# A TensorE branch for experts of at most 32 tokens in layer 0 of a mixture-of-experts trunk, with ScalarE copying the first product's sums

## The chip, the cores and the metric

The kernel runs on one core of a Trainium2 chip. The metric is the device time of one execution in microseconds (us). A core has TensorE (PE; its weight loads are listed apart as PEld), VectorE (DVE), ScalarE (ACT), GpSimd (POOL) and SyncE (SP), which run their own instruction queues and wait for one another by semaphores; sixteen DMA engines move data between the core's memory and HBM.

## What is computed

The kernel computes a trunk of two layers on 1024 tokens of width 1024: a pooling mixer (layer 0) and a gated linear attention (layer 1), each followed by a mixture of 64 experts. Each token goes to the best of 8 groups and, in it, to the best two of 8 experts; an expert is a gated MLP with 384 hidden columns. Cut to the part around the change:

```python
def hier_moe(h, w_group, b_group, w_expert, b_expert, w_in, w_out):
    ...
    p_g, g_idx = lax.top_k(p_group, 1)
    ...
    p_top, e_idx = lax.top_k(p_e, MOE_TOP_E)
    weights = p_g * p_top / jnp.sum(p_top, axis=-1, keepdims=True)
    flat_id = (g_idx * MOE_EXPERTS_PER_GROUP + e_idx).reshape(-1)
    order = jnp.argsort(flat_id)
    token_of = order // MOE_TOP_E
    xs = t[token_of]
    group_sizes = jnp.bincount(flat_id, length=MOE_EXPERTS).astype(jnp.int32)
    gu = lax.ragged_dot(xs, w_in, group_sizes)
    gate, up = jnp.split(gu, 2, axis=-1)
    ys = lax.ragged_dot(jax.nn.silu(gate) * up, w_out, group_sizes)
    ys = ys * weights.reshape(-1)[order][:, None].astype(ys.dtype)
    out = jnp.zeros_like(t).at[token_of].add(ys)
```

A layer adds `gate2 * hier_moe(...)` to its input. 2048 pairs of token and expert are shared by 64 experts, 32 each on average; the weights of one expert are 1024x768 and 384x1024 float32, 4.7 MB.

## The kernel before

Layer 0 first makes its modulation vectors (`rows_use`, line 172: stationary 128x32, moving 128x384, sums on four groups of 32 PSUM partitions, one after the other), the pooling mixer and the routing. Then `moe` (line 624) goes over the experts, in layer 0 with the groups sorted by their number of tokens. The loop body names an expert by its position e, 0 to 63.

For each expert, up to 64 token rows are gathered (`gather`, 516, on GpSimd, two experts ahead, half rows of 512 columns on 128 partitions, so that 64 tokens fill them). `expert_in` (523) turns them with four TensorE transposes (528) and scales them into `xT` on ScalarE and VectorE (536, 538). `expert_first` (546) makes the first product: 16 matmuls of 128x384 with 64 stationary columns (64 tokens), gate columns of w_in into one half of the PSUM partitions and up columns into the other (554). The trace has two records for each such float32 matmul, hence 32. `expert_hidden` (558) is Silu of the gate half on ScalarE (561) and the product with the up half on VectorE (562). `expert_turn` (564) is three transposes (570) and a ScalarE copy (571). `expert_last` (573) is the product with w_out: six matmuls of 128x512, 12 records (579). `expert_add` (583) scales on VectorE (584) and adds the rows to `x_d` in HBM by an indirect DMA on GpSimd (585).

In layer 0, `expert_out` (590) puts TensorE's work in this order, which is kept as written: first product, the next expert's transposes (`between`), two filler units, the turn, two units, last product, four units. A unit (`piece`, 954) is three float16 matmuls of 128x512 (973) of layer 1's input projection; eight units make a 128x512 block that ScalarE evicts (975) and GpSimd's queue writes to HBM (976). Units exist from position 18 on, and run out now and then, before the next tile of 128 tokens is ready for them. Positions 2 to 15 have none and go through `expert_either` (602), as all experts of layer 1 do. Positions 0, 1 and 16 to 63 go through `expert_out`. After it, all engines but SyncE read the expert's count and branch (680): over 64 tokens, a second pass follows; otherwise it is jumped over, and TensorE adds what the pass would have added to its semaphore.

The weights of an expert take three of six slots of 1.5 MB (two for w_in, one for w_out), loaded by SyncE (`third_load`, 507, lines 513 and 514). The loads of expert e + 2 stand behind the branch of expert e, and each also waits for the load three before it.

Of the kernel before, what the change touches and what calls it, by code (L numbers as in the profile page):

```python
# [11 lines left out]
AF = mybir.ActivationFunctionType  # L12
OP = mybir.AluOpType
# [23 lines left out]
def trunk_kernel(ctx, tc, x_in, c_in, norm_gain, w_mod, b_mod, pool_w, pool_b, pool_scale,  # L37
# [20 lines left out]
    def part(slot, kb, n):  # L58
        a = int(kb * 256)
        return A[slot][:, a:a + n]  # L60

    def ps():
        return psum.tile([128, 512], F32, name="ps")
# [23 lines left out]
    cnt_i = cv(88)[0:1, :].bitcast(I32)  # L87
    wz_, isc_ = cv(128), cv(128)
    wz = wz_.rearrange("p (a b) -> p a b", a=8)
    zst = part(15, 11.25, 32).rearrange("p (b f) -> p b f", b=2)  # L90
    ig = cv(128).rearrange("p (a b) -> p a b", a=2).bitcast(I32)
    isc = isc_.rearrange("p (a b) -> p a b", a=2).bitcast(I32)
    wsl = cv(128).rearrange("p (a b) -> p a b", a=2)
# [1 line left out]
    so = small[:, 58:66].bitcast(I32)  # L95
    G2 = cv(512)
    gs = part(15, 11.5, 40)
    gmax, ginv, gmul, gadd = (gs[:, 8 * i:8 * i + 8] for i in range(4))
    gout = gs[:, 32:33]
    gtmp = gs[:, 33:37]  # L100
# [195 lines left out]
    def route_consts(area):  # L296

        ones_b, trim = as16(area("ones", 64)), as16(area("trim", 64))
        V.memset(ones_b, 1.0)
        V.tensor_tensor(trim, slot_no, pno.to_broadcast([128, 128]), op=OP.is_le)  # L300
        V.tensor_scalar(trim, trim, -1.0, None, op0=OP.mult)
        return ones_b, trim
# [220 lines left out]
    def expert_in(l, i, g, first=None):  # L523
        xT = part(15, 2 * i, 512).rearrange("p (c g t) -> p c g t", c=4, g=2)
        pp = [ps(), ps()]
        for cc in range(4):
            rows = XG[g].rearrange("p (r c) -> p c r", c=4)[:, cc] if l else XG[g][:, cc * 128:(cc + 1) * 128]
            T.transpose(pp[cc % 2][:, cc // 2 * 128:cc // 2 * 128 + 128], rows, ident)  # L528
        with tc.issue_after(first()) if first else ExitStack():
            for cc in range(4):  # L530
                pv = pp[cc % 2][:, cc // 2 * 128:cc // 2 * 128 + 128].rearrange("p (g t) -> p g t", g=2)
                for g in range(2):
                    kc = 4 * g + cc
                    sc, sh = modA[:, 0, 1, kc:kc + 1], sec(0, 3)[:, kc:kc + 1]
                    if cc % 2:
                        S.activation(xT[:, cc, g, :], pv[:, g, :], AF.Identity, bias=sh, scale=sc)  # L536
                    else:
                        ins = V.tensor_scalar(xT[:, cc, g, :], pv[:, g, :], sc, sh, op0=OP.mult, op1=OP.add).ins  # L538
        return ins
# [50 lines left out]
    def expert_out(l, i, sl, to, y, between=None, fill=lambda n: None):  # L590
        p1 = expert_first(i, sl)
        if between:
            between()
        fill(2)
        mark[:] = [expert_hidden(i, p1)]
        mark.append(expert_turn(i))
        fill(2)
        p2 = expert_last(i, sl)
        fill(4)
        expert_add(l, p2, *to, y)  # L600

    def expert_either(l, i, sl, to, y, nxt, many, to2, y2, aside):

        def hidden(b, p, n):
            if n:
                return expert_in(l, n[0], n[1], lambda: expert_hidden(b, p))
            return expert_hidden(b, p)

        p1 = expert_first(i, sl)
        with tc.If(many) as cmp:  # L610
            ins = hidden(i, p1, (i, y2))
            aside(ins, expert_turn(i))
            p2 = expert_last(i, sl)
            p1b = expert_first(i, sl, 1 - i)
            expert_add(l, p2, *to, y)
            hidden(1 - i, p1b, nxt)
            expert_turn(1 - i)
            expert_add(l, expert_last(1 - i, sl), *to2, y2)
        with cmp.Else():
            ins = hidden(i, p1, nxt)  # L620
            aside(ins, expert_turn(i))
            expert_add(l, expert_last(i, sl), *to, y)

    def moe(l, ring, mb, ob, load, ng, na, filler=None, before=None, aside=None, after=None):


        nr = len(ring)
        to = ig if l else isc
        pool_only = (ET.Pool,)

        def slots_at(e):
            return [ring[(3 * e + j) % nr] for j in range(3)]

        def count(e, engines):
            return nc.values_load(cnt_i[0:1, e:e + 1], engines=engines, min_val=0, max_val=SEQ,
                                  skip_runtime_bounds_check_because=COUNT_REASON)

        def main(e):
            return mb[e % len(mb)]

        def more(e):
            return ob[e % len(ob)]

        def ahead(e):
            if e < NE:
                with tc.If(count(e, pool_only) > 64):
                    gather(ig[:, 1, e:e + 1], more(e))

        for e in range(na):
            ahead(e)  # L650
        expert_in(l, 0, main(0))
        for e in range(NE):
            i = e % 2
            sl = slots_at(e)

            def between():
                if e + 1 < NE:
                    expert_in(l, 1 - i, main(e + 1))

            if before:  # L660
                before(e)
            if e + ng < NE:
                gather(ig[:, 0, e + ng:e + ng + 1], main(e + ng))
            tos = [(wsl[:, k, e:e + 1], to[:, k, e:e + 1]) for k in range(2)]
            engines = (ET.Pool, ET.Activation, ET.PE, ET.DVE)
            if l or 1 < e < NE // 4 and not units:
                ahead(e + na)
                expert_either(l, i, sl, tos[0], main(e), (1 - i, main(e + 1)) if e + 1 < NE else None,
                              count(e, engines) > 64, tos[1], more(e), aside or (lambda *marks: None))
                if after:  # L670
                    after(e)
            else:
                expert_out(l, i, sl, tos[0], main(e), between,
                           (lambda n: filler(e, n)) if filler else (lambda n: None))
                if aside:
                    aside(*mark)
                if after:
                    after(e)
                ahead(e + na)
                with tc.If(count(e, engines) > 64):  # L680
                    expert_in(l, i, more(e))
                    expert_out(l, i, sl, tos[1], more(e))
            for s in range(nr + 3 * e, min(nr + 3 * e + 3, 3 * NE)):
                load(s // 3, s % 3, slots_at(s // 3))
# [156 lines left out]
    def urgent(r):  # L841
        with tc.high_priority():
            next(r)
            next(r)
        next(r)

    urgent(route(0, 0, NT, area0, route_consts(area0)))
    gather(ig[:, 0, 0:1], 0)
    last = gather(ig[:, 0, 1:2], 1)
# [138 lines left out]
    def filler(e, n):  # L988
        if e < NE - 1:
            run_units(min(n, len(units) - 32) if e > NE - 6 else n)  # L990
# [474 lines left out]
```

## Time and profile before

| | us |
|---|---|
| median of 3 runs | 2311.88 |
| lowest and highest | 2305.32 to 2315.17 |
| the profiled execution | 2305.41 |
| its span, first to last instruction | 2303.7 |
| its granted TensorE clock, mean | 0.967 |

| engine | busy us | share of the span |
|---|---|---|
| PE | 1982.4 | 86% |
| PEld | 952.9 | 41% |
| DVE | 719.3 | 31% |
| ACT | 617.9 | 27% |
| POOL | 498.7 | 22% |

The busy time of an engine is the union of its instructions' times. The ends of matmuls are modelled, and records of matmuls overlap: the time from one start to the next is less than a record's duration. Branches, register loads and waits of an engine's sequencer aren't counted as busy; they are marked by a q (PEldq is TensorE's). A slice of the page is 57.6 us.

### The profile page before, as it was taken

The page shows a single profiled execution, that of the slowest core. Times are in us where ns is not written, and L with a number is a line of the kernel's source. Part 1 is how long each engine was busy: PE and PEld are TensorE (multiplying, and loading weights), DVE is VectorE, ACT ScalarE, POOL GpSimd, SP SyncE. Part 2 cuts the span into 40 slices and gives each one's busy share as a digit, 9 for nine tenths or more (in the row PEclk, how much of TensorE's full clock was granted, in tenths as well). Part 3 has the DMA queues.
Part 4 walks back from the last instruction along what each step waited for, and adds up shares of the span by engine and source line. Part 5 has one row for each costly group of instructions (what it writes and reads, how often), then busy time and mean ns, then how long its engine had stood idle before and what let it go on. Part 6 is the DMA issues. An engine that isn't in the chain of part 4 may idle for free. (4 is left out here: it accounts for less than half of the span.)

```text
span 2303.7 us, 31289 instructions
## 1 busy us (share of the span) xinstructions
PE 1982.4 (86%) x11197; PEld 952.9 (41%) x11198; DVE 719.3 (31%) x1760; ACT 617.9 (27%) x1418; POOL 498.7 (22%) x425
## 2 busy tenths in 40 slices
PE   7958888899999999998988999888887777778894
PEld 5644333344444444444434566533333333333341
DVE  3454545212111221211237666622221211122122
ACT  4222323222212221212125666312111111111113
POOL 0303222222222222222115110122222212122211
PEclk9979999999999999999998999999999999999997
DMA  9979989998988998999954952699999999999995
GB/s 349 365 302 383 394 302 345 373 341 326 347 309 296 336 359 321 369 337 360 349 169 143 332 192 89 238 388 406 406 398 392 404 388 402 396 398 389 400 385 191
DMA packets 173511, 770.07 MB, mean 334 GB/s; under 512 B 31711, under 2 KB 41357, under 8 KB 136382
## 3 DMA queue, kind: packets, MB, share of 16 engines
q1 hardware_dynamic: 127922, 684.66, 74.9%
q0 software_dynamic: 43952, 77.69, 12.3%
q10 hardware_dynamic: 1372, 4.28, 0.5%
q8 instruction: 155, 2.54, 0.4%
q14 instruction: 110, 0.90, 0.1%
HBM read 735.45 MB, written 69.80 MB: 350 GB/s over the span
## 5 line engine op out<-in xcount | busy, mean ns | idle before, releaser
L554 PE MATMUL ps<-slot,slot 128*64 128x384 f32 x4416 | 751.2, 490 | 77.2 <-DMA slot<-in_moe_w_in_dram 57.7
L554 PEld LDWEIGHTS ps<-slot,slot 128*64 128x64 f32 x4416 | 334.9, 137 | 494.9 <-issue 266.7
L579 PE MATMUL ps<-slot,slot 128*64 128x512 f32 x1656 | 403.3, 624 | 50.0 <-ACT slot L571 47.5
L561 ACT ACTIVATE slot<-ps 64x384 f32<-64x384 f32 x138 | 66.9, 485 | 1237.1 <-PE ps L554 1208.2
L973 PE MATMUL ps<-slot,slot 128*128 128x512 f16 x1152 | 278.9, 389 | 8.9 <-PEq L1110 5.6
L585 POOL DMA_INDIRECT x_d<-kept x96 | 159.4, 1661 | 544.5 <-DVEq L680 172.7
L538 DVE TENSOR_SCALAR slot<-ps,kept 128x64 f32<-128x64 f32 x552 | 151.1, 334 | 339.5 <-PE ps L528 338.1
L562 DVE TENSOR_TENSOR slot<-slot,ps 64x384 f32<-64x384 f32 x138 | 75.9, 550 | 504.9 <-ACT slot L561 504.2
L579 PEld LDWEIGHTS ps<-slot,slot 128*64 128x64 f32 x1656 | 110.7, 141 | 249.1 <-issue 183.8
L536 ACT ACTIVATE slot<-ps,kept 128x64 f32<-128x64 f32 x552 | 177.9, 402 | 66.5 <-PE ps L528 64.5
L584 DVE SCALAR_TENSOR_TENSOR kept<-ps,kept 128x512 f32<-128x512 f32 x96 | 72.0, 750 | 326.6 <-PE ps L579 323.8
L973 PEld LDWEIGHTS <-slot 128*128 128x128 f16 x1152 | 108.1, 100 | 156.6 <-issue 50.3
L517 POOL DMA_INDIRECT kept<-h_d,kept x96 | 102.2, 1065 | 307.4 <-DMA x_d<-kept 189.2
L570 PE MATMUL ps<-kept,slot 64*128 64x64 f32 x414 | 75.9, 290 | 85.7 <-DVE slot L562 84.2
L585 POOL DMA_INDIRECT x_d<-slot,kept x42 | 66.9, 1592 | 352.2 <-DVE slot L584 158.3
L570 PEld LDWEIGHTS ps<-kept,slot 64*128 64x128 f32 x414 | 57.9, 202 | 126.3 <-DVE slot L562 93.1
L1285 PE MATMUL ps<-slot,slot 128*128 128x512 f16 x384 | 85.7, 379 | 1.2 <-DVE slot L1277 0.9
L584 DVE SCALAR_TENSOR_TENSOR slot<-ps,kept 128x512 f32<-128x512 f32 x42 | 31.5, 751 | 124.3 <-PE ps L579 118.3
L528 PEld LDWEIGHTS ps<-kept 128*128 128x128 f32 x384 | 44.6, 163 | 61.4 <-issue 60.8
L528 PE MATMUL ps<-kept 128*128 128x128 f32 x384 | 65.8, 294 | 4.5 <-DMA kept<-h_d,kept 4.5
L1285 PEld LDWEIGHTS <-slot 128*128 128x128 f16 x384 | 37.1, 98 | 46.7 <-issue 2.1
L571 ACT COPY slot<-ps 128x192 f32<-128x192 f32 x138 | 44.6, 323 | 32.1 <-PE ps L570 32.1
(343 smaller groups left out, 1681.9 us busy)
## 6 DMA issues: line engine op xcount, KB each, us to landing
slot<-in_moe_w_in_dram SPq DMA_DIRECT2D x256, 1536.0 KB, 12.3
slot<-in_moe_w_out_dram SPq DMA_DIRECT2D x128, 1536.0 KB, 12.8
slot<-in_w_mod_dram SPq DMA_DIRECT2D x24, 1536.0 KB, 11.2
slot<-in_gla_w_in_dram SPq DMA_DIRECT2D x8, 1536.0 KB, 8.4
slot<-in_w_mod_dram SPq DMA_DIRECT2D x8, 1152.0 KB, 7.8
h_d<-slot POOLq DMA_DIRECT2D x16, 512.0 KB, 5.7
slot<-in_x_dram SPq DMA_DIRECT2D x8, 512.0 KB, 11.6
slot<-x_d POOLq DMA_DIRECT2D x8, 512.0 KB, 7.5
```

The source lines that it names most:

```text
L517: return G.indirect_dma_start(out=XG[i], out_offset=None, in_=hv, in_offset=bass.IndirectOffsetOnAxis(ap=idx, axis=0), bounds_check=2 * SE ...
L528: T.transpose(pp[cc % 2][:, cc // 2 * 128:cc // 2 * 128 + 128], rows, ident)
L536: S.activation(xT[:, cc, g, :], pv[:, g, :], AF.Identity, bias=sh, scale=sc)
L538: ins = V.tensor_scalar(xT[:, cc, g, :], pv[:, g, :], sc, sh, op0=OP.mult, op1=OP.add).ins
L554: T.matmul(p1[s, 0:384], xT[:, cc, g, :], W[:, u], start=n == 0, stop=n == 7)
L562: return V.tensor_tensor(hh, hh, p1[up, 0:384], op=OP.mult).ins
L570: T.transpose(p3[:, cc * 64:(cc + 1) * 64], hh[:, :, cc], ident[s, s])
L579: T.matmul(p2[g * 64:g * 64 + 64, :], hT[:, cc * 64:(cc + 1) * 64], o[:, cc, g * 512:(g + 1) * 512], start=cc == 0, stop=cc == 2)
L584: V.scalar_tensor_tensor(XG[y], p2, w, G2, op0=OP.mult, op1=OP.mult)
L585: ins = G.indirect_dma_start(out=yv[l], out_offset=bass.IndirectOffsetOnAxis(ap=sidx, axis=0), in_=XG[y], in_offset=None, bounds_check=2 * ...
L973: T.matmul(p, hP[:, m, kc, :], W[:, n, :], start=kc + i == 0, stop=kc == KC - 1 and i == 2)
L1285: T.matmul(p, oT[:, m, kc, :], woh[kc][:, n, half * 512:(half + 1) * 512], start=kc + i == 0, stop=kc == KC - 1 and i == 2)
```

## The change

In layer 0, `expert_out`'s first pass becomes `expert_few`. On TensorE alone, the count of the expert is compared with 32 twice. With at most 32 tokens, the first product uses 32 stationary columns and four groups of 32 PSUM partitions (gate and up, each with its even and odd parts of the contraction); otherwise it is done as before. ScalarE copies the 128x384 sums to SBUF (`pc`), ahead of the next expert's scaling. The turn is made of the sums, not of the hidden rows: with at most 32 tokens by three matmuls with the matrix `pick`, which adds even and odd parts while it turns; otherwise by three transposes. Silu (ScalarE) and the product (VectorE) then work on the turned sums, 128x192. Second passes, `expert_either` and layer 1 stay as they are. `pick` is made once; a small staging buffer (`zst`) moves to another place.

```diff
-    zst = part(15, 11.25, 32).rearrange("p (b f) -> p b f", b=2)
+    zst = part(15, 11.6875, 32).rearrange("p (b f) -> p b f", b=2)
...
+    pick = part(15, 11, 128)
...
+    def first_of(few, i, sl):
+        p1 = ps()
+        xT = part(15, 2 * i, 512).rearrange("p (c g t) -> p c g t", c=4, g=2)
+
+        def weights(g, cc, u):
+            return A[sl[g]].rearrange("p (k u f) -> p k u f", k=4, u=2)[:, cc, u]
+
+        with tc.If(few) as cmp:
+            for n in range(4):
+                for u in range(2):
+                    for odd in range(2):
+                        g, cc = n // 2, n % 2 * 2 + odd
+                        q = 32 * (2 * u + odd)
+                        T.matmul(p1[q:q + 32, 0:384], xT[:, cc, g, 0:32], weights(g, cc, u), start=n == 0, stop=n == 3)
+        with cmp.Else():
+            for n in range(8):
+                for u in range(2):
+                    T.matmul(p1[64 * u:64 * u + 64, 0:384], xT[:, n % 4, n // 4, :], weights(n // 4, n % 4, u),
+                             start=n == 0, stop=n == 7)
+        return p1
+
+    def turn_of(few, b, pc):
+        pv = pc.rearrange("p (r c) -> p r c", c=3)
+        hT = part(15, 5.5 + 0.75 * b, 192).rearrange("p (c t) -> p c t", c=3)
+        p3 = ps()
+        with tc.If(few) as cmp:
+            for cc in range(3):
+                T.matmul(p3[:, cc * 128:(cc + 1) * 128], pv[:, :, cc], pick, start=True, stop=True)
+        with cmp.Else():
+            for cc in range(3):
+                T.transpose(p3[:, cc * 128:(cc + 1) * 128], pv[:, :, cc], ident)
+        p3v = p3[:, 0:384].rearrange("p (c u t) -> p c u t", c=3, u=2)
+        S.activation(hT, p3v[:, :, 0], AF.Silu)
+        return V.tensor_tensor(hT, hT, p3v[:, :, 1], op=OP.mult).ins
+
+    def expert_few(l, i, sl, to, y, few, between, fill):
+        p1 = first_of(few, i, sl)
+        pc = part(15, 4, 384)
+
+        def copy():
+            mark[:] = [S.copy(pc, p1[:, 0:384]).ins]
+            return mark[0]
+
+        between(copy)
+        fill(2)
+        mark.append(turn_of(few, i, pc))
+        fill(2)
+        p2 = expert_last(i, sl)
+        fill(4)
+        expert_add(l, p2, *to, y)
...
+        few = {}
+
+        def few_next(e):
+            if e < NE and e not in few:
+                few[e] = count(e, (ET.PE,)) <= 32
...
-            def between():
+            def between(first):
                 if e + 1 < NE:
-                    expert_in(l, 1 - i, main(e + 1))
+                    expert_in(l, 1 - i, main(e + 1), first)
+                else:
+                    first()
...
-                expert_out(l, i, sl, tos[0], main(e), between,
-                           (lambda n: filler(e, n)) if filler else (lambda n: None))
+                few_next(e)
+                expert_few(l, i, sl, tos[0], main(e), few.pop(e), between, lambda n: filler(e, n))
...
                 ahead(e + na)
+                few_next(e + 1)
                 with tc.If(count(e, engines) > 64):
...
+    V.memset(pick, 0.0)
+    sides_of = "p (u h t) -> p u h t"
+    V.tensor_tensor(pick.rearrange(sides_of, u=2, h=2)[:, :, 0], ident.rearrange(sides_of, u=2, h=2)[:, :, 0],
+                    ident.rearrange(sides_of, u=2, h=2)[:, :, 1], op=OP.add)
```

## Rows read from the trace of the kernel before

**Rows 1.** The page: an engine's busy time, and GB/s in 40 slices.
```profile
PE 1982.4 (86%) x11197; PEld 952.9 (41%) x11198; DVE 719.3 (31%) x1760; ACT 617.9 (27%) x1418; POOL 498.7 (22%) x425
...
GB/s 349 365 302 383 394 302 345 373 341 326 347 309 296 336 359 321 369 337 360 349 169 143 332 192 89 238 388 406 406 398 392 404 388 402 396 398 389 400 385 191
```

**Rows 2.** Stretches: length, each engine's busy time, granted clock, DMA share, GB/s.
```profile
250.00:300.00 50.00, 40.03 (x217) 16.89 (x219) 25.92 (x50) 15.88 (x35) 13.23 (x10) 1.00 1.02 387
452.40:1149.60 697.20, 656.96 (x3420) 296.15 (x3420) 135.82 (x343) 162.19 (x397) 156.02 (x142) 0.99 0.91 337
468.60:529.80 61.20, 58.51 (x300) 25.69 (x301) 10.40 (x27) 14.77 (x35) 14.18 (x13) 1.00 0.94 348
1600.00:1700.00 100.00, 90.02 (x503) 39.57 (x499) 22.11 (x56) 18.35 (x56) 23.79 (x18) 1.00 1.01 403
```

**Rows 3.** Timeline of PE, one expert with units: start, us, instructions, idle before.
```profile
483.82 5.38 PE L554 MATMUL ps<-slot,slot 128*64 128x384 f32 x32 [0.30 <-PEq L680]
489.13 0.66 PE L528 MATMUL ps<-kept 128*128 128x128 f32 x4
489.62 1.46 PE L973 MATMUL ps<-slot,slot 128*128 128x512 f16 x6
491.55 0.53 PE L570 MATMUL ps<-kept,slot 64*128 64x64 f32 x3 [0.47 <-DVE slot L562]
492.01 1.47 PE L973 MATMUL ps<-slot,slot 128*128 128x512 f16 x6
493.41 2.79 PE L579 MATMUL ps<-slot,slot 128*64 128x512 f32 x12
496.14 2.76 PE L973 MATMUL ps<-slot,slot 128*128 128x512 f16 x12
499.20 1.19 PE L554 MATMUL ps<-slot,slot 128*64 128x384 f32 x6 [0.30 <-PEq L680]
```

**Rows 4.** PE's waits, 452.4 to 1149.6 us: total us, times, longest.
```profile
PE ps L570 <- DVE slot L562: 23.2, 44, 1.8
PE ps L554 <- PEq L680: 12.5, 42, 0.4
```

**Rows 5.** DMA issues and median landing, 452.4 to 1149.6; last two: 250 to 300.
```profile
slot<-in_moe_w_in_dram SPq DMA_DIRECT2D x90, 1536.0 KB, 9.4
...
x_d<-kept POOLq DMA_INDIRECT x45, 4.9
kept<-h_d,kept POOLq DMA_INDIRECT x44, 6.4
...
kept<-h_d,kept POOLq DMA_INDIRECT x4, 7.8
x_d<-kept POOLq DMA_INDIRECT x3, 8.0
```

**Rows 6.** Waits of SyncE's queue, 452.4 to 1149.6 us.
```profile
SPq L513 <- PEq L680: 317.4, 44, 14.4
```

**Rows 7.** Timeline of PE: one burst of modulation matmuls (line 180).
```profile
81.89 2.79 PE L180 MATMUL ps<-slot,slot 128*32 128x384 f32 x32
```

**Rows 8.** Timeline of PE: full matmuls of 128 columns in the pooling mixer.
```profile
16.52 2.23 PE L783 MATMUL ps<-slot,slot 128*128 128x128 f32 x14
```

**Rows 9.** Lines 610 and 680, TensorE's branches: ns min/median/max, first and last start.
```profile
L610 PEldq COMPARE_BRANCH  x87: 65/213/361, 214.9 to 2268.4; - x87
L680 PEldq COMPARE_BRANCH  x51: 70/217/360, 192.8 to 1157.8; - x51
```

**Rows 10.** Groups by line, ACT, whole span: copies from PSUM.
```profile
L571 ACT COPY slot<-ps 128x192 f32<-128x192 f32 x138 | 44.6, 323 | 32.1 <-PE ps L570 32.1
L187 ACT COPY slot<-ps 128x384 f32<-128x384 f32 x5 | 2.3, 478 | 18.7 <-PE ps L180 18.7
```

**Rows 11.** Timeline of PE: positions 49 (three filler matmuls) and 51, the starts.
```profile
948.66 5.38 PE L554 MATMUL ps<-slot,slot 128*64 128x384 f32 x32 [0.30 <-PEq L680]
...
974.78 1.51 PE L554 MATMUL ps<-slot,slot 128*64 128x384 f32 x8 [0.30 <-PEq L680]
```

## The prediction

> **What bounds the kernel now.** I read the page first: TensorE is busy for 86% of the span, and the memory traffic runs near 400 GB/s in the last third but mostly between 300 and 380 in slices 6 to 20, where layer 0's experts run [rows 1]. The table of stretches separates the two: in layer 1 (1600 to 1700 us) the transfers are full (share 1.01, 403 GB/s) and TensorE has gaps; while layer 0 mixes experts with filler matmuls (452.4 to 1149.6 us), TensorE is busy for 657 of 697 us at a granted clock of 0.99 and the transfers stand at a share of 0.91 and 337 GB/s [rows 2]. So this stretch is TensorE's, with a small reserve in the transfers. The timeline of one expert there is its whole budget [rows 3]: first product 5.31 us (483.82 to 489.13), transposes 0.49, two filler units with a wait of 0.47, the turn of the hidden rows 0.46, two units 1.40, the last product 2.73, four units and a gap of 0.30, together 15.38 us. Of TensorE's waits in the stretch two matter: 23.2 us for the hidden product on VectorE, 12.5 us at the end of an expert [rows 4]. The weights don't make it wait: a half of w_in lands 9.4 us after its issue [rows 5], and SyncE issues an expert's loads only when TensorE leaves the expert two before it (317.4 us of waiting in 44 times) [rows 6], so that they have one expert's length, 15.4 us, and arrive some 6 us early.
>
> **How many experts change.** The new code serves positions 0, 1 and 16 to 63. The reference's routing of its own inputs, sorted by group size as the kernel sorts them, gives at most 32 tokens at 38 of these 50: 18, 20, 21, 23 to 30, 32 to 38, 40, 42 to 50, 53, 55 to 63, all in the stretch. Of the 38, 30 have all filler units; 42, 49, 50, 57, 58, 61, 62 and 63 have nearly none. Twelve of the 50 take the other branch.
>
> **First product.** 32 records stay 32 records of 384 columns, on four column groups instead of two. The trace has that very form: the modulation matmuls of line 180, 32 records of 128x384 with 32 weight columns, cycling through the four groups as the new loop does, took 2.79 us, three times alike, against 5.38 [rows 3, 7]. Saving: 2.59 us. The Trainium skill's page "TensorE: Matmul & The Clock Gate", section "Part 3: Packing small matmuls", lists measured speedups of 3.07 for four row tiles and 2.38 for three column tiles, less than the number of tiles. By 3.07 against a full two, the product would take an estimated 3.5 us and save 1.9; the row of the same form speaks against it here, and no run yet shows the form inside an expert.
>
> **Turn.** The small branch has three full matmuls of 128 columns, six records instead of three. Fourteen records of that form took 2.23 us [rows 8], 0.112 us from one to the next, so six cost 0.67 against 0.46: +0.21. The other branch's three transposes of 128 columns are one record each, about +0.05.
>
> **Two branches on TensorE.** Branches on its queue took 65 to 361 ns: the low end where the code falls through, the high one where it jumps [rows 9]. The count's register load comes before the old branch, which TensorE's queue covers. The first branch stands right behind the old one's end, where TensorE has run empty (the 0.30 gap), so it is exposed: 0.17 us for the fall-through of small experts (0.07 and one step), 0.4 for the jump of the others; between 0 and 0.4. The jump at the end of the body and the second branch have filler or product work queued ahead: 0. If that cover is gone, 0.3 each. Does the end of a branch empty TensorE, as that of the old one does? That one adds to TensorE's own semaphore because its skipped side has fewer matmuls; here both sides have as many (16, and 3), so I take 0, with 0.4 for each of the two as the upper bound.
>
> **The path from first to last product.** Today: Silu, four VectorE scalings, the product, the turn, a copy. New: a copy of 128x384 (478 ns), then the turn; and behind it Silu and product on 128x192, some 323 ns each by the copy of that size [rows 10]. The first part, 0.48 and two handovers, is covered by transposes and two units (1.9 us); so the wait of 0.24 to 0.5 per expert goes: -0.3. The second, about 0.9 us, is covered by two units (1.40); without units it shows 0.5 more than the copy's 0.41 of today. The copy waits where the Silu waited, with the four scalings and, at times, a unit's eviction behind it on ScalarE; the next one waiting for those is the next expert's first product, a dozen us away. The scalings on VectorE no longer stand ahead of what TensorE waits for. The matrix pick is made once, by two VectorE instructions ahead of the routing, and a small buffer moves to free its place: at most 1 us on the whole. No transfer and no SyncE or GpSimd step is moved in the code; but loads start when TensorE leaves an expert, so they start sooner.
>
> **Small expert with filler, TensorE alone:** -2.59 + 0.21 + 0.17 - 0.3 = -2.5 us, from 15.4 to 12.9. The others: +0.4 - 0.3, about 0.
>
> **What is late next: the transfers.** Four such experts moved 348 GB/s x 61.2 us = 21.3 MB, 5.3 MB each [rows 2]. At the 387 GB/s of layer 0's own full stretch (250 to 300 us) that is 13.8 us, at layer 1's 403 it is 13.2; by the share, 0.94 of 15.3 us at a full 1.02, it is 14.1. I take 13.7. So 12.9 can't be held: each expert eats 0.8 us of the lead, which is 12.9 - 9.4 = 3.5 us [rows 5], and after four in a row the transfers set the pace. The 30 stand in runs of 1, 2, 8, 7, 1, 6, 1, 2 and 2: 21 in the first four of a run (2.5 each: 52 us), 9 behind (1.7 each: 15). The eight without units take 13.1 us now (two of them 948.66 to 974.78) [rows 11], about the transfers' own need (5.0 MB at 390 GB/s is 12.8): 2 us in all, at most 20. Sum 69. From the other side: 697 us at a share of 0.91 can't fall below 622 at 1.02, 75 us; the eight larger experts between 18 and 63 go on at 15.4 with about 1.2 us idle transfers each, leaving 65. Both can't be met without loss where the two engines alternate; I take 60 us, nearer the cap. The profiled execution took 2305.4 us (span 2303.7 and 1.7 around it), 6.5 under the median of three, 2311.9; 60 off it is 2245, and off the median 2252.
>
> **Rivals.**
> 1. The branches' ends empty TensorE: 0.8 more per expert. The small ones then take 13.7, where the transfers would hold many of them anyway: 30 x 1.7 less 12 x 0.8 is 41 us, 2271. For: the 0.30 gap behind the old branch. Against: equal counts.
> 2. The gathers come late. An expert's row gather is issued only after the scatter-add of the expert three before it has landed; the landings are 4.9 and 6.4 us, 8.0 and 7.8 when the transfers are full [rows 5], so 15.8 with some 1.5 for issuing. The rows are needed 1.5 + 12.9 + 2.8 = 17.2 us after that scatter-add starts: just met. A us late on each of 30 costs 30: 2282. Spills on GpSimd's queue stand in between.
> 3. Slower: the jumps stall on code. If one jump in three (some 33 of 100) waited for code as long as the shortest landing, 4.9 us, that is 162 us lost against 60: 2414; it decides from 0.6 us per jump. Against: the old branches jump over a whole second pass in at most 0.36 us [rows 9]. The Trainium skill's page "Runtime: NRT & Kernel Launch", section "Instruction fetch mechanics", has this rule: a taken branch whose target lies outside the fetched window waits for a transfer. Its effect isn't seen in these rows.
> 4. The change doesn't do what it says: hardly any expert takes the small side, or the groups don't overlap there. Then 50 x 0.1 to 0.4 is lost, 2317 to 2332, or the gain is below 12.
> 5. The transfers do better than today's share says (403 GB/s throughout): 85 us, 2227.
>
> **Chances:** forecast 0.64 (2234 to 2267), rival 1 0.12, rival 2 0.10, rival 3 0.04, rival 4 0.07, rival 5 0.03. About 0.5% (12 us) can be told from no change. Faster by more: forecast, 1, 2 and 5 less a little for their tails, 0.87; within: 0.07; slower: 0.06. The range takes in rivals 1, 2 and nearly 5: 2230 to 2293.
>
> **What would show it.** Small experts: the first product as 32 records of 32 weight columns in about 2.8 us, the whole expert in 12.9 to 13.7; larger ones 5.4 and 15.4. Within runs of small experts, waits of the first product for w_in or of the transposes for gathers appear, the share rises to about 1.0, and the wait for VectorE at the turn vanishes in experts with units. The next layer stays as it is. Wrong would be: a first product above 3.5 us, gaps of over 0.5 us behind either branch, or a stretch whose share stays at 0.91 while TensorE waits.

## The result, and the profile after

The changed kernel took 2258.0 us (median of 4 runs, 2251.0 to 2265.5) against 2308.6 for the kernel before beside it (4 runs): a ratio of 0.977, interval 0.975 to 0.980, 51 us faster. Predicted were 2252, with 2230 to 2293 around it. The profiled execution took 2258.2 us with a span of 2256.5, 47.2 less than before's.

In its profile line 618 is the first product of a small expert (at most 32 tokens) and 622 that of a larger one; 633 and 636 are their turns, 646 the copy of the sums, 638 Silu, 639 the product, 580 the last product, 1041 a filler unit, 1043 ScalarE's eviction of a filler block, 744 the old branch, 612 and 631 the two new ones.

TensorE's timeline shows a small expert with units, and further up two rows of a larger one; the columns are those of [rows 3]:

```profile
473.45 5.38 PE L622 MATMUL ps<-slot,slot 128*64 128x384 f32 x32 [0.58 <-PEq L744]
...
481.22 0.61 PE L636 MATMUL ps<-kept,slot 128*128 128x128 f32 x3 [0.50 <-ACT slot L646]
...
575.35 2.79 PE L618 MATMUL ps<-slot,slot 128*32 128x384 f32 x32 [0.48 <-PEq L744]
578.07 0.65 PE L529 MATMUL ps<-kept 128*128 128x128 f32 x4
578.56 1.46 PE L1041 MATMUL ps<-slot,slot 128*128 128x512 f16 x6
580.52 1.31 PE L633 MATMUL ps<-slot 128*128 128x128 f32 x6 [0.50 <-ACT slot L646]
581.66 1.46 PE L1041 MATMUL ps<-slot,slot 128*128 128x512 f16 x6
583.05 2.79 PE L580 MATMUL ps<-slot,slot 128*64 128x512 f32 x12
585.78 2.76 PE L1041 MATMUL ps<-slot,slot 128*128 128x512 f16 x12
588.97 1.50 PE L618 MATMUL ps<-slot,slot 128*32 128x384 f32 x16 [0.42 <-PEq L744]
```

From start to start, against [rows 3]:

| step | before, us | after, us | predicted change | change |
|---|---|---|---|---|
| first product | 5.31 | 2.72 | -2.59 | -2.59 |
| transposes | 0.49 | 0.49 | 0 | 0 |
| two units and the wait at the turn | 1.93 | 1.96 | -0.3 | +0.03 |
| turn | 0.46 | 1.14 | +0.21 | +0.68 |
| two units | 1.40 | 1.39 | 0 | -0.01 |
| last product | 2.73 | 2.73 | 0 | 0 |
| four units and the gap at the end | 3.06 | 3.19 | +0.17 | +0.13 |
| sum | 15.38 | 13.62 | -2.5 | -1.76 |

So the first product came as computed, and so did the branch. The turn cost three times its surcharge, and the wait in front of it is still there; only the one who is waited for has changed, from VectorE's hidden product to ScalarE's copy. TensorE's waits in the stretch say it for all experts (columns as in [rows 4]; then the stretch itself, columns as in [rows 2]):

```profile
PE ps L633 <- ACT slot L646: 19.2, 30, 1.3
PE ps L618 <- PEq L744: 14.3, 33, 0.5
PE ps L580 <- DVE slot L639: 13.4, 11, 2.6
PE ps L618 <- DMA slot<-in_moe_w_in_dram: 5.6, 6, 2.3
...
PE ps L636 <- ACT slot L646: 3.5, 7, 0.5
```

```profile
452.00:1110.00 658.00, 594.12 (x3581) 269.75 (x3581) 130.19 (x345) 167.55 (x407) 158.37 (x144) 0.98 0.97 363
```

The transfers went from a share of 0.91 to 0.97 and from 337 to 363 GB/s [rows 2], but the first product waited for weights only 6 times, 5.6 us together. SyncE's queue waited for the old branch for 317.4 us before [rows 6] and now does so for less. It also waits for earlier loads to land, as it did before. First a row of the kernel before (452.4 to 1149.6 us), then two of the kernel after (452 to 1110):

```profile
SPq L513 <- DMA slot<-in_moe_w_in_dram: 239.7, 44, 7.3
```

```profile
SPq L514 <- PEq L744: 247.6, 44, 12.6
SPq L514 <- DMA slot<-in_moe_w_in_dram: 217.8, 51, 8.2
```

**Why the turn waits and is long.** ScalarE's timeline in the same expert, and two groups of instructions by line (busy us, mean ns of one, idle before):

```profile
579.41 0.69 ACT L1043 ACTIVATE slot<-ps,slot 128x512 f32<-128x512 f32 x1 [10.88 <-PE ps L1041]
579.99 0.47 ACT L646 COPY slot<-ps 128x384 f32<-128x384 f32 x1
580.35 1.31 ACT L537 ACTIVATE slot<-ps,kept 128x64 f32<-128x64 f32 x4
581.86 0.33 ACT L638 ACTIVATE slot<-ps 128x192 f32<-128x192 f32 x1 [0.21 <-issue]
```

```profile
L633 PEld LDWEIGHTS ps<-slot 128*128 128x128 f32 x228 | 42.9, 260 | 35.9 <-ACT slot L646 35.2
L646 ACT COPY slot<-ps 128x384 f32<-128x384 f32 x50 | 23.6, 473 | 51.2 <-PE ps L622 29.5 <-PE ps L618 20.2 <-PE ps L529 1.4
```

ScalarE has stood idle for 10.9 us, and the sums have been there since 578.1. But its queue holds the eviction of a filler block first, which must wait for the units behind the transposes; the copy comes behind it, 1.85 us after the sums, though in the code it stands ahead. So it is in 24 of the 30 small experts with units; in the other six no block is completed there. And each weight load of the turn takes 260 ns: `pc` is read with a step of three elements. The costs of the branches are small, as predicted:

```profile
L612 PEldq COMPARE_BRANCH  x88: 67/176/1256, 185.7 to 1108.0; - x88
```

**Where the 47 us are.** By the starts of the first products in the two profiles:

| part | before, us | after, us | change |
|---|---|---|---|
| ahead of position 0 | 183.4 | 190.2 | +6.8 |
| positions 0 and 1 | 29.0 | 28.0 | -1.0 |
| positions 2 to 15 | 212.5 | 213.4 | +0.9 |
| positions 16 to 62 | 724.7 | 672.6 | -52.1 |
| position 63 and all behind it | 1154.1 | 1152.4 | -1.7 |

Of the 52.1, the 30 small experts with units hold -55.4 (1.85 each), the eight larger ones +1.5, the seven small ones without units +1.4, positions 16 and 17 +0.4. The 6.8 ahead of position 0 belong to that one execution: in the profiles of the eight experiments below, with the same code there, position 0 starts at 171.9 to 182.5 us.

### The profile page after: what moved, and what is told of

It is laid out like the page before. It is cut to its first block, busy times and chain, and to the rows that moved or that the text cites. A ratio compares the mean times of both kernels' runs of the same rounds, so it can differ in the third digit from the quotient of the medians.

```text
span 2256.5 us, 31745 instructions
## 1 busy us (share of the span) xinstructions
PE 1912.5 (85%) x11311; PEld 924.9 (41%) x11312; DVE 710.4 (31%) x1762; ACT 621.8 (28%) x1425; POOL 498.6 (22%) x425
## 3 DMA queue, kind: packets, MB, share of 16 engines
q8 instruction: 170, 2.79, 0.5%
## 5 line engine op out<-in xcount | busy, mean ns | idle before, releaser
L555 PE MATMUL ps<-slot,slot 128*64 128x384 f32 x2816 | 482.2, 491 | 63.7 <-DMA slot<-in_moe_w_in_dram 58.3
L555 PEld LDWEIGHTS ps<-slot,slot 128*64 128x64 f32 x2816 | 204.9, 138 | 350.3 <-issue 233.2
L1041 PE MATMUL ps<-slot,slot 128*128 128x512 f16 x1152 | 273.5, 383 | 7.3 <-DVEq L1178 5.8
L562 ACT ACTIVATE slot<-ps 64x384 f32<-64x384 f32 x88 | 42.7, 485 | 753.9 <-PE ps L555 718.1
L580 PEld LDWEIGHTS ps<-slot,slot 128*64 128x64 f32 x1656 | 111.5, 141 | 264.1 <-issue 169.9
L563 DVE TENSOR_TENSOR slot<-slot,ps 64x384 f32<-64x384 f32 x88 | 48.6, 552 | 499.5 <-ACT slot L562 494.5
L1041 PEld LDWEIGHTS <-slot 128*128 128x128 f16 x1152 | 112.4, 101 | 150.5 <-issue 44.6
L1043 ACT ACTIVATE slot<-ps,slot 128x512 f32<-128x512 f32 x48 | 32.7, 686 | 415.3 <-PE ps L1041 409.4
L618 PE MATMUL ps<-slot,slot 128*32 128x384 f32 x1216 | 107.2, 488 | 21.3 <-PEq L744 14.3
L571 PE MATMUL ps<-kept,slot 64*128 64x64 f32 x264 | 49.0, 293 | 56.0 <-DVE slot L563 53.0
L1353 PE MATMUL ps<-slot,slot 128*128 128x512 f16 x384 | 85.7, 379 | 1.2 <-DVE slot L1345 0.9
L618 PEld LDWEIGHTS ps<-slot,slot 128*32 128x32 f32 x1216 | 42.6, 109 | 79.0 <-issue 64.3
L622 PE MATMUL ps<-slot,slot 128*64 128x384 f32 x384 | 66.7, 501 | 9.0 <-PEq L744 5.5
```

The costliest lines, as they stand in the source:

```text
L555: T.matmul(p1[s, 0:384], xT[:, cc, g, :], W[:, u], start=n == 0, stop=n == 7)
L571: T.transpose(p3[:, cc * 64:(cc + 1) * 64], hh[:, :, cc], ident[s, s])
L580: T.matmul(p2[g * 64:g * 64 + 64, :], hT[:, cc * 64:(cc + 1) * 64], o[:, cc, g * 512:(g + 1) * 512], start=cc == 0, stop=cc == 2)
L618: T.matmul(p1[q:q + 32, 0:384], xT[:, cc, g, 0:32], weights(g, cc, u), start=n == 0, stop=n == 3)
L622: T.matmul(p1[64 * u:64 * u + 64, 0:384], xT[:, n % 4, n // 4, :], weights(n // 4, n % 4, u), start=n == 0, stop=n == 7)
L1041: T.matmul(p, hP[:, m, kc, :], W[:, n, :], start=kc + i == 0, stop=kc == KC - 1 and i == 2)
```

## Experiments

Each ratio is against the kernel before on the same chip (2303.9 us, 10 runs, for the first four; 2306.7, 11 runs, for the others). Beside the kernel after it took 2308.6, so differences between kernels are given by the ratios below (0.001 is 2.3 us), not by the medians. They carry about 10 us either way; the stretch and the clean expert, each from one profile, are finer. "Stretch" is from the first product of position 16 to that of 63; "clean expert" is a small expert with units in which nothing else waits.

| kernel | median, us | ratio, 95% interval | stretch, us | clean expert, us |
|---|---|---|---|---|
| before | 2308.6 | | 724.7 | 15.38 |
| after | 2258.0 | 0.977 (0.975 to 0.980) | 672.6 | 13.62 |
| e1_wide | 2329.2 | 1.010 (1.006 to 1.013) | 753.2 | 15.67 |
| e2_copy_late | 2289.5 | 0.992 (0.989 to 0.995) | 713.9 | 14.22 |
| e3_evict_after | 2231.0 | 0.968 (0.964 to 0.972) | 655.6 | 12.79 |
| e4_contig | 2240.2 | 0.970 (0.966 to 0.975) | 659.9 | 13.24 |
| e5_both | 2227.5 | 0.967 (0.964 to 0.969) | 649.7 | 12.48 |
| e6_no_if | 2210.0 | 0.961 (0.957 to 0.964) | 628.8 | 12.35 |
| e7_half_out | 2194.8 | 0.954 (0.951 to 0.957) | 635.2 | 12.48 |
| e8_old_start | 2222.5 | 0.966 (0.963 to 0.968) | 647.9 | 12.48 |

**e1_wide: the new arrangement without the four groups.** All 50 experts take the other side (1600 records of line 622, none of 618).

```diff
-                few[e] = count(e, (ET.PE,)) <= 32
+                few[e] = count(e, (ET.PE,)) <= 2
```

> The limit of the small branch is set to 2 tokens, so that every expert at positions 0, 1 and 16 to 63 takes the branch with 64 columns: the new arrangement (two branches on TensorE, the copy, the turn of the sums) without the four column groups. If the gain is the four groups alone, this is no faster than the kernel before (2308.6 us): the larger experts of the changed kernel took 0.1 to 0.3 us more each than before, 50 times that is 5 to 15, so 2305 to 2325. The rival, that ScalarE's earlier copy and the shorter work behind it bring part of the gain, wants under 2295.

Measured: 2329.2 us, by the ratio 22 us more than before. TensorE's timeline has the reason, in an expert that was small in the kernel after:

```profile
567.43 5.38 PE L622 MATMUL ps<-slot,slot 128*64 128x384 f32 x32 [0.69 <-PEq L744]
...
575.19 0.62 PE L636 MATMUL ps<-kept,slot 128*128 128x128 f32 x3 [0.50 <-ACT slot L646]
...
583.10 5.38 PE L622 MATMUL ps<-slot,slot 128*64 128x384 f32 x32 [0.57 <-PEq L744]
```

15.67 us from start to start: the exposed jump adds 0.27 to 0.39 to the old gap of 0.30, and the 0.50 in front of the turn is about what it was (0.47) [rows 3]. The copy ahead of the scalings, the sums in the turn and the two branches bring nothing by themselves; all the gain is the four column groups', some 75 us of it (1.010 to 0.977).

**e2_copy_late: the copy behind the next expert's scalings.**

```diff
-        between(copy)
+        between(None)
+        copy()
```

> The changed kernel, with ScalarE's copy of the sums behind the scaling of the next expert's rows. If the scalings in front delay the copy, the wait of the turn grows from 0.50 to about 1.1 us in each of some 37 experts with filler units, 2275 to 2285 us against 2258. The rival, that the copy is held by the eviction of a filler block in front of it and not by the scalings, wants no change: 2253 to 2263.

Measured: 2289.5, by the ratios 35 us more than the kernel after, above the expected band. The profiles' stretch grew by 41.3 us; 24.5 of them lie in the 30 small experts with units, the rest in others, which the expectation hadn't counted. ScalarE's timeline shows the order, TensorE's waits the price:

```profile
540.86 1.29 ACT L537 ACTIVATE slot<-ps,kept 128x64 f32<-128x64 f32 x4 [10.25 <-PE ps L529]
542.03 0.70 ACT L1042 ACTIVATE slot<-ps,slot 128x512 f32<-128x512 f32 x1
542.60 0.50 ACT L646 COPY slot<-ps 128x384 f32<-128x384 f32 x1
```

```profile
PE ps L633 <- ACT slot L646: 44.5, 32, 3.1
```

The wait at the turn grows from 19.2 us in 30 to 44.5 in 32. So the copy's place on ScalarE's queue is worth much, and this version again has the eviction ahead of the copy. That pointed to the next one.

**e3_evict_after: only the eviction moves behind the copy.** The planner is told to issue a filler block's eviction after the expert's copy.

```diff
+            copied[:] = mark[:]
...
-                S.activation(stg[b % 2], p, AF.Copy, scale=gout)
+                with tc.issue_after(copied[0]) if copied else ExitStack():
+                    S.activation(stg[b % 2], p, AF.Copy, scale=gout)
```

> The changed kernel, with the eviction of a filler block (128x512, 0.69 us on ScalarE) queued behind the copy of the sums instead of ahead of it. If that eviction is what the turn's wait of 0.50 us comes from, the wait goes and small experts with units take 13.1 us: 37 x 0.5 = 18 us less, 2240. The rival, that the transfers already set the pace (13.2 to 14.1 us an expert, as predicted), turns it into waits for w_in: 2252 to 2260.

Measured: 2231.0, by the ratios 21 us under the kernel after (18 expected); the profiles' stretch is 17.0 shorter. The rival (transfers take it back) falls in the main: the 30 small experts with units give 16.0 us more than in the kernel after, and the seven without lose 4.3. TensorE's timeline from the units to the turn, then its waits (634 is the turn, 619 the first product, 647 the copy here):

```profile
550.34 1.46 PE L1043 MATMUL ps<-slot,slot 128*128 128x512 f16 x6
551.63 1.15 PE L634 MATMUL ps<-slot 128*128 128x128 f32 x6
552.62 1.46 PE L1043 MATMUL ps<-slot,slot 128*128 128x512 f16 x6
```

```profile
PE ps L619 <- DMA slot<-in_moe_w_in_dram: 16.1, 10, 3.2
...
PE ps L634 <- ACT slot L647: 3.6, 4, 1.2
```

The clean expert falls by 0.83, more than the 0.50 that the trace put down as the wait: units to turn 1.96 to 1.29 (0.67), and the turn 1.14 to 0.99. The 0.67 are the idle 0.50 and an overlap of 0.17: the turn now starts before the units' last record ends (551.63 against 551.80). The rest is the turn's first weight load, which now starts 0.21 us ahead of the turn's first matmul (551.42 against 551.63), beside the units; behind the wait it starts together with that matmul (580.51 against 580.52). At the same time the waits for weights go from 5.6 to 16.1 us: now the transfers can be seen.

**e4_contig: the copy writes the sums in the order in which the turn reads them.** The stride moves from TensorE's weight load to ScalarE's write.

```diff
-        pv = pc.rearrange("p (r c) -> p r c", c=3)
+        pv = pc.rearrange("p (c r) -> p c r", c=3)
...
-            mark[:] = [S.copy(pc, p1[:, 0:384]).ins]
+            mark[:] = [S.copy(pc.rearrange("p (c r) -> p c r", c=3), p1[:, 0:384].rearrange("p (r c) -> p c r", c=3)).ins]
```

> The changed kernel, with the copied sums laid out so that each of the turn's three stationary matrices is contiguous (ScalarE reads PSUM with the stride of three instead). If the stride of the weights is what makes the turn's six records stand 0.174 us apart instead of the 0.112 of contiguous ones, the turn falls from 1.14 to about 0.7 us: 38 x 0.45 = 17 us less, 2241, unless ScalarE's copy grows. The rival, that the spacing comes from elsewhere, wants 0.174 again and 2258.

Measured: 2240.2, by the ratios 16 us under the kernel after (17 expected); the profiles' stretch is 12.7 shorter. TensorE's timeline at the turn, and the weight loads by line:

```profile
573.95 0.94 PE L633 MATMUL ps<-slot 128*128 128x128 f32 x6 [0.50 <-ACT slot L646]
574.73 1.46 PE L1041 MATMUL ps<-slot,slot 128*128 128x512 f16 x6
```

```profile
L633 PEld LDWEIGHTS ps<-slot 128*128 128x128 f32 x228 | 29.4, 194 | 36.7 <-ACT slot L646 35.8
```

The load is 194 ns instead of 260, the turn 0.78 instead of 1.14, and ScalarE's copy is no longer for its new stride (474 ns against 473). The wait of 0.50 stays: the two causes are separate.

**e5_both: e3_evict_after and e4_contig together.** Its diff is the two above.

> The eviction of a filler block behind the copy (as in e3_evict_after) and the sums copied so that the turn reads them in one piece (as in e4_contig), together. Theory A, TensorE sets the pace of the stretch: both gains add, 27 + 18 us off the changed kernel's 2258, 2213 us (2206 to 2220); a small expert with units takes 12.4 us, its turn six records in about 0.67 us, without the wait for the copy. Theory B, the transfers stop it: the stretch is already at a DMA share of 0.99 in e3_evict_after, so nothing more comes out than there, 2226 to 2234 us, small experts stay at 12.8, and the 0.4 us that the turn gives back reappear as waits of the first product for w_in or of the transposes for the gathered rows.

Measured: 2227.5; by the ratios 24 us under the kernel after (0.967 against 0.977), where the two alone gave 21 and 16. Its interval overlaps that of e3_evict_after, so the times alone don't tell these two apart. TensorE's timeline in an expert (581 is the last product), its waits, and four stretches: nearly all of it, positions 32 to 38, the first two of these, and the other five:

```profile
653.54 2.79 PE L619 MATMUL ps<-slot,slot 128*32 128x384 f32 x32
656.26 0.66 PE L530 MATMUL ps<-kept 128*128 128x128 f32 x4
656.75 1.46 PE L1043 MATMUL ps<-slot,slot 128*128 128x512 f16 x6
658.04 0.83 PE L634 MATMUL ps<-slot 128*128 128x128 f32 x6
658.71 1.46 PE L1043 MATMUL ps<-slot,slot 128*128 128x512 f16 x6
...
666.01 1.45 PE L619 MATMUL ps<-slot,slot 128*32 128x384 f32 x13 [0.42 <-PEq L746]
```

```profile
PE ps L619 <- DMA slot<-in_moe_w_in_dram: 16.5, 11, 3.0
PE ps L581 <- DVE slot L640: 14.8, 8, 2.9
```

```profile
452.00:1070.00 618.00, 558.25 (x3491) 250.43 (x3494) 124.95 (x333) 164.12 (x395) 152.35 (x142) 0.99 1.00 377
653.50:745.60 92.10, 87.34 (x572) 39.50 (x571) 19.98 (x53) 26.64 (x63) 26.08 (x24) 1.00 0.97 365
653.54:678.49 24.95, 24.11 (x158) 10.45 (x157) 6.14 (x16) 8.15 (x20) 8.34 (x8) 1.00 0.85 310
678.49:745.60 67.11, 63.19 (x414) 29.05 (x415) 13.83 (x37) 18.49 (x43) 17.74 (x17) 1.00 1.02 386
```

Here the turn is 0.67 (658.04 to 658.71), the prediction's own term, there is no wait, and the clean expert takes 12.47. Neither theory holds alone: the median lies in B's band, but not for B's reason alone. The 30 small experts with units give 77.0 us against before, 21.6 more than in the kernel after (e3_evict_after 16.0 more, e4_contig 8.9: nearly the sum). Positions 32 to 38, seven small ones in a row, take 92.1 us without one wait of the first product for w_in (second row): A holds there, though not for long. The first two find loads that came early, behind the two passes of position 31 (25.4 us), and the transfers stand at a share of 0.85; in the other five the transfers are full (1.02). And the seven experts without units now take 5.7 us more than before instead of 1.4, mostly with w_in as what they wait for, and the stretch is at a share of 1.00: B holds there.

The later eviction also has a price. ScalarE changes its table of functions now and then (1.28 us); in the kernel after the eviction or the copy meets that change, here it is always the copy (7 times in 50). At positions 21, 27 and 34 the last product then waits 1.57 us for Silu and product, 0.62 in the kernel after.

**e6_no_if: no branches, every expert with 32 columns.**

```diff
-        with tc.If(few) as cmp:
+        if True:
...
-                few[e] = count(e, (ET.PE,)) <= 32
+                few[e] = None
```

> As e5_both without the two branches on TensorE: every expert of the new arrangement takes 32 stationary columns (the tokens from 33 on to 64 of an expert are left out). Theory A, TensorE sets the pace: eight larger experts between positions 18 and 63 give 2.7 us each, 22 us, positions 0, 1, 16 and 17 some 10, and 50 first branches 0.12 each, 6: 38 us under e5_both, 2175 if that is at 2213. Theory B, the transfers set it: at most 10 us under e5_both, from positions 0, 1, 16 and 17, and the first products wait for w_in. If the branches cost more than their gap (0.12 us), small experts get shorter here by more than that.

Measured: 2210.0, 14 us under e5_both by the ratios: between A (38) and B (10). First the start of an expert on TensorE's timeline, then its waits and the stretch:

```profile
670.84 1.50 PE L619 MATMUL ps<-slot,slot 128*32 128x384 f32 x16 [0.30 <-PEq L738]
```

```profile
PE ps L619 <- DMA slot<-in_moe_w_in_dram: 22.6, 21, 3.4
```

```profile
452.00:1070.00 618.00, 557.45 (x3562) 244.97 (x3560) 126.57 (x334) 166.75 (x395) 156.63 (x144) 0.97 1.00 386
```

Without branches the clean expert is 12.35 instead of 12.48: the two branches together cost the 0.12 by which the gap at the end of an expert had grown (0.42 to 0.30), and nothing in the middle. The larger experts give up 15.7 us against e5_both (19.7 against 4.0 under before) of A's 22; the small ones lose 0.9, and the first product now waits for weights 21 times.

**e7_half_out: e5_both with half of w_out.**

```diff
+        if l == 0:
+            return [queued(SP.dma_start(A[sl[2]][:, 0:768], wout.rearrange("(p c) d -> p (c d)", c=3)[:, 0:768]))]
```

> As e5_both, but layer 0 loads only the first half of each expert's w_out (the second half is left out, and the product uses what lies there): 0.79 of some 5.3 MB less per expert. The span falls in any case by what positions 2 to 15 gain, which run at full transfers (14 x 0.79 MB at 387 GB/s: up to 28 us), so the stretch of positions 18 to 63 is what counts. Theory A, TensorE sets the pace there: small experts with units as in e5_both, within 0.15 us. Theory B, the transfers set it: they get shorter by up to 2 us, down to 12.3, and the waits for w_in go.

Measured: 2194.8, by the ratios 29 us under e5_both. Of the profile's 26.4 us less span, 14.5 lie in the stretch. TensorE's waits (621 is the first product here) and the stretch:

```profile
PE ps L621 <- DMA slot<-in_moe_w_in_dram: 4.8, 5, 1.9
```

```profile
452.00:1070.00 618.00, 567.33 (x3558) 254.73 (x3557) 128.61 (x337) 164.61 (x394) 157.49 (x145) 0.99 0.85 300
```

With the share down to 0.85 the waits for w_in fall from 16.5 to 4.8 us, and the clean expert stays at 12.48, as A says. From position 18 to 49, where nearly all have units, e7_half_out is only 3.7 us shorter than e5_both (428.4 against 432.1); from 49 to 63, where most have none, 11.5 (178.2 against 189.7). So in e5_both the transfers cost at least about 4 us where units fill TensorE, and about three times that where they don't.

**e8_old_start: e5_both with the old arrangement at positions 0, 1, 16 and 17.**

```diff
+                if e < 18:
+                    expert_out(l, i, sl, tos[0], main(e), lambda: expert_in(l, 1 - i, main(e + 1)),
+                               lambda n: filler(e, n))
```

> As e5_both, but positions 0, 1, 16 and 17, which have no filler units ahead of or behind their turn (16 and 17) or none at all (0 and 1), keep the old arrangement: Silu and product on the rows, then the turn, and no branch. Theory: in the new one Silu and product stand between the turn and the last product and nothing covers them there; the profiles show 2 to 4 us more at position 0 and up to 2.5 at the others, so 4 to 8 us under e5_both. Rival: these positions wait for transfers anyway, so no change (within 2 us), and position 2 begins at the same time.

Measured: 2222.5, with an interval that overlaps that of e5_both. By the traces the rival holds: positions 0 and 1 take 27.7 us in e5_both and 27.6 here, 16 and 17 take 27.9 and 27.8. In the new arrangement the last product does wait there for Silu and product (1.5 to 2.9 us each), but in the old one the turn waits instead (1.5 to 1.8 us each), what position 0 loses (1.9) position 1 has less (1.8), what 17 loses (2.0) 16 has less (2.0), and position 2 waits 2.56 us for its weights in both. So these positions cost the change nothing. Of the kernels that compute everything this one, e5_both and e3_evict_after are the fastest, by the ratios 21 to 27 us under the changed kernel, and their intervals overlap.

## Why the prediction came out where it did

**Right: what bounds the kernel, and the first product.** The stretch was TensorE's, and a cut on TensorE came through. 32 records of 32 columns on four groups took 2.79 us as those of line 180 did [rows 7]; the estimate of 3.5 us by the factor 3.07 that the Trainium skill gives for four row tiles ("TensorE: Matmul & The Clock Gate", "Part 3: Packing small matmuls") was too high for these four column groups. 38 experts took the small side (1216 records of line 618, 32 each), as counted. e1_wide shows that this is the whole gain.

**Right: the branches.** The exposed one costs 0.12 at a small expert (0.17 predicted) and 0.28 at a larger one (0.58 less 0.30; 0.4 predicted), the second nothing, and their ends don't empty TensorE: rival 1 is out by the timeline and by e6_no_if. The larger experts' gap of 0.58 is just past the prediction's sign of being wrong (over 0.5), but 0.30 of it was there before. Rival 3 is out as well: the branches of line 612 have a median of 176 ns, and the 1256 above stands alone, the next longest being 427. What held that one up isn't shown; it lies behind queued matmuls of position 35, which takes 15.15 us, as its like 29 does (15.14). The rule of "Runtime: NRT & Kernel Launch", "Instruction fetch mechanics", in the Trainium skill, of a wait at a jump out of the fetched window, has no price here that these rows show.

**Wrong: the wait at the turn.** The step said that the copy "is covered by transposes and two units (1.9 us); so the wait of 0.24 to 0.5 per expert goes: -0.3". The length of the cover was right, the start of the copy wasn't. I had placed it where the Silu stood, with evictions "at times" behind it; in the changed kernel's queue the eviction of the block that those very units complete stands ahead of it in 24 of the 30 small experts with units, so that the copy can't start before the cover is used up. e3_evict_after, which changes that order alone, takes the wait away (19.2 us in 30 times in the kernel after, 3.6 in 4 there): 21 us by the ratios, 17 in the stretch.

**Wrong in size: the turn.** +0.21 was read from full matmuls of 128 columns with 0.112 us from one to the next [rows 8]. Those load their weights from consecutive elements; `pv` steps by three. The load takes 260 ns instead of 194, and six of them behind an empty queue 1.14 us instead of 0.67. e4_contig and e5_both bring 0.78 (behind the wait) and 0.67 (without it): the term was right for the form that I had priced, and the form was another. The stride is in the diff (`"p (r c) -> p r c", c=3`), and a row of the same shape says nothing of it.

**Wrong in what sets the pace, though the number fits: the transfers as the next bound.** Forecast were 12.9 us by TensorE and, since that "can't be held", a pace of 13.7 by the transfers. The 13.62 measured is TensorE's own: 12.87 as summed up there, 0.33 and 0.47 more by the two errors above, 0.04 less at the branch and 0.01 in the units. In the kernel after, the first product waited for w_in for 5.6 us in 658. That the two numbers agree is luck.

The price itself was about right. In e5_both positions 34 to 38 moved 386 GB/s for 67.1 us at a share of 1.02, which is 5.2 MB and 13.4 us each, against 5.3 and 13.7 in the prediction. The mean of the seven from 32 on (365 GB/s, 4.8 MB each) is less only because part of their weights had come before. So a lead is used up by small experts, as the prediction says; but an expert that takes longer gives some back, as position 31 did, and a cap after four in a row was too strict. 77.0 us from the 30 small experts in e5_both are 2.57 each, TensorE's -2.5 in full, where I had capped them at 67. Nor is the floor by the share a floor: 622 us for positions 18 to 62 is what e5_both takes (621.9, from 447.58 to 1069.43), but e6_no_if takes 605.0 (445.78 to 1050.74).

My reading of the lead before left out that SyncE's queue also waited for earlier loads (239.7 us in 44 times, above): the 9.4 us are the median over single halves of w_in, not the way of an expert's three loads.

The bound exists: the small side's first products wait for w_in longer as the kernels get faster, 5.6 us over the whole run in the kernel after, 9.1 in e4_contig, 16.1 in e3_evict_after, 18.8 in e5_both and 22.6 in e6_no_if, where all 50 experts take that side; e7_half_out takes most of it away (4.8). It binds mostly in the experts without units, where TensorE has little to hide a load behind.

**Nearly right: the others.** The eight larger experts: 0 predicted, +1.5 in sum. The small ones without units, from 42 on: -2 predicted, +1.4 in sum; their last product waits for Silu and product, 0.81 us in four of the seven, about the predicted 0.91, and 1.9 in three, where ScalarE loads its table of functions ahead of Silu (1.28 us). Gathers held TensorE up once, among positions 2 to 15 (4.6 us; 2.8 at the same place before, and 3.1 once more at position 1), and nowhere in the stretch: rival 2 is out.

The sum: 55.4 instead of 67 from the small experts with units, the rest near zero; 60 predicted, 51 measured by the medians. What was missed on the turn and its wait (0.33 + 0.47 us per small expert with units, 24 us) was in part made up by what was wrongly taken off for the transfers (30 x 2.5 is 75, and 60 was forecast). That 2252 came so near to 2258 is owed to these two errors against each other.

## What to carry to other kernels

To price a moved step, write down the queue of its engine as the planner will order it, by readiness and not by lines of code, and look at what stands directly ahead of it: here one eviction ahead of one copy cost some 20 us (21 by the ratios, 17 in the stretch), all the branches some 8 (38 x 0.12 + 12 x 0.28). Price an instruction by a row with the same access pattern, not only the same shape; the stride can often be moved to an engine where it costs nothing. And a bound by bandwidth acts through a lead: before it caps a sum, ask how early the loads stand when a run of short experts begins and what gives the lead back. The bytes that pass in a window are what its experts need only where the loads stand as early at its end as at its start.

## What the runs showed of the hardware that I had not expected

- A weight load of 128x128 float32 that steps by three elements takes 260 ns, one of consecutive elements 194 (e4_contig); ScalarE's copy out of PSUM takes 473 to 474 ns whichever of the two it writes.
- An idle time of 0.50 us in front of six short matmuls cost 0.8 us on TensorE's path (e3_evict_after against after): 0.17 of overlap with the matmul ahead, and 0.15 behind the first load of weights, which had nothing to run beside.
- Four column groups with float32 operands give nearly their full factor over two: 5.38 to 2.79 us for 32 records, inside an expert as in a burst of their own.
- Branches on TensorE whose two sides hold equally many matmuls did not empty it: 0.12 us for the two of a small expert, all of it in the gap at the end of an expert that was there before (e6_no_if).
- A share of 1.00 of the DMA engines did not fix the rate: from 452 to 1070 us it went with 377 GB/s in e5_both and with 386 in e6_no_if.
